# Summing, norming and multiplying each tile of tokens on its own between two transformer blocks

## The chip, the cores and the metric

The kernel runs on one core of a Trainium2 chip. The metric is the device time of one execution in microseconds (us), the median of several runs. The engines are named as the profile names them: PE (TensorE, matmuls), PEld (its weight loads), DVE (VectorE), ACT (ScalarE), POOL (GpSimd) and SP (SyncE, which issues the DMAs here). Each engine works through its own instructions in order and waits for others at semaphores.

## What is computed

The program is two transformer blocks over 512 tokens of width 1024: a block with two attentions and a mixture of experts, then a block with three other attentions and an MLP. All of it is float32. What matters here lies between the two blocks:

```python
    x = x + gate_f * moe_ffn(h, ...)          # end of the first block
    return rms_norm(x, g_final)
...
    h = rms_norm_2(x, norm_mix[l])            # start of the second block
    proj = h @ w_in[l]
```

where both norms are `x * rsqrt(mean(x*x) + 1e-6) * gain`. So x is normed twice in a row, and the result is multiplied by `w_in`.

## The kernel before

Tokens lie in four tiles of 128 (the variable `c` or `i`). The residual x is `xres`, four tiles of 128x1024 in SBUF. Products that need precision are written as three matmuls in a rounded format (`mm3`, lines 121 to 123): a value is kept as a rounded part `hi`, made by ACT (line 88), and a remainder `lo`, made by DVE (line 89); the matmuls are hi*hi, hi*lo and lo*hi. Of a weight these parts are the tiles `whi` and `wlo`, three buffers each; the raw weights are loaded by SP into `raw`, three buffers.

The experts are worked off in slots (the loop of `phase_b`). For each slot the program makes y, 128 rows of expert output, as `yh` and `yl` (line 1073 multiplies by the gate, lines 88 and 89 split), and a selection matrix S. `combine` (lines 1084 to 1094) adds S^T y to `xres`: for each tile and each half of 512 columns it runs two matmuls per slot into one PSUM bank and one addition on DVE. Of the last two slots the sums are made in `tail`. The last slot's y lies in a buffer named `rawh`, so its products read `rawh`; its matmuls of line 1071 work on four experts of 32 rows.

`tail` takes the tiles in pairs. It sums both, squares them on ACT (line 1486) and weights the squares on DVE (line 1488), finds both norms' scales with a Newton iteration in small DVE instructions (lines 1490 to 1495, 262 to 267), multiplies each tile by its scale and gains (line 1499), turns it by eight PE transposes (line 1504) and splits it into `c_hh` and `c_hl`. The four instructions of line 1510 write the normed x back. The products with the first 396 columns of `w_in_2` come later, in `nsa_kv` of `phase_c`: for each quarter of the 1024 rows of the weight it runs over all four tiles. Then ACT and DVE read them (`kvc`, `kvt`, `ksw`, `gt`), PE turns `ksw` (line 1667), and the query's products (`nsa_q`, lines 121 to 123 on `c_hh` with 512 columns) follow. Masks and gains are loaded into `mkf`, `gains` and others at the start of `phase_c`.

A scheduler sets each engine's order when the program is built, from its own estimate of when each instruction is ready. `order(a, b)` forces b behind a on the same engine. `pe` does that for every matmul that is passed to it while `self.chain` is a list; so PE's order in the expert loop is the order of the code.

Of the kernel before, what the change touches and what calls it, by code (L numbers as in the profile page):

```python
# [11 lines left out]
F32 = mybir.dt.float32  # L12
F32R = mybir.dt.float32r
# [45 lines left out]
class Kern:  # L59
# [750 lines left out]
    NB = sum(k[0] for k in KINDS)  # L810
# [284 lines left out]

    def phase_b(self):
        nc, tc, I = self.nc, self.tc, self.I
        xr, hT, hp = self.xres, self.h2T, self.hp
        E, STAT, NB, NS, NF = self.E, self.STAT, self.NB, self.NS, self.NF
# [57 lines left out]
        for j in range(3):  # L1157
            t = rt.tile([128, D], F32, name=f"xg{j}")
# [13 lines left out]
        for c in range(NCH):  # L1172
# [4 lines left out]
                                       op0=OP.add, op1=OP.mult)  # L1177
# [56 lines left out]
        for name, src in (("pos", pos), ("gate", sco)):  # L1234
            t = self.tps()
# [4 lines left out]
            t = self.tps()  # L1240
# [72 lines left out]
        n = 2  # L1313
        while todo:
            p = todo[0]
# [4 lines left out]
            n = 3  # L1320
# [144 lines left out]
        self.gains = g[:, :D], g[:, D:]  # L1465
        self.rowcast(self.gains[0], I["g_final"].rearrange("(o d) -> o d", o=1))
        self.rowcast(self.gains[1], I["norm_mix_2"])
        nc.gpsimd.tensor_tensor(self.gains[1], self.gains[0], self.gains[1], op=OP.mult)

        nc.gpsimd.tensor_tensor(self.gff, self.gains[0], self.gains[0], op=OP.mult)  # L1470
        self.done, self.ex = done, ex
        bwx.close()

    def tail(self):

        nc, xr, hT = self.nc, self.xres, self.cT
        gfin, gmix = self.gains
        G = 2
        sq2, xn2 = [self.hold.tile([128, self.RAW], F32, name="rawh", bufs=self.NP) for _ in range(2)]
        for a in range(0, NCH, G):  # L1480
            self.combine(self.done, range(a, a + G))
            st = self.nst[:, a * 6:(a + G) * 6].rearrange("p (s n) -> p s n", s=6)
            xs = [xr[:, a + j, :] for j in range(G)]
            for j in range(G):
                sq = sq2[:, (a + j) % 2 * D:][:, :D]
                d = nc.scalar.activation(sq, xs[j], AF.Square, accum_out=st[:, 0, j:j + 1])
                self.order(self.pin, d)
                nc.vector.scalar_tensor_tensor(sq, sq, 1.0, self.gff, op0=OP.mult, op1=OP.mult, accum_out=st[:, 1, j:j + 1])

            nc.vector.tensor_scalar(st[:, 0], st[:, 0], 1.0 / D, EPS, op0=OP.mult, op1=OP.add)  # L1490
            nc.vector.reciprocal(st[:, 2], st[:, 0])
            nc.vector.scalar_tensor_tensor(st[:, 1], st[:, 1], 1.0 / D, st[:, 2], op0=OP.mult, op1=OP.mult)
            nc.vector.tensor_scalar(st[:, 1], st[:, 1], EPS, None, op0=OP.add)
            self.rsqrt(st[:, 4:6], st[:, 0:2], st[:, 2:4])
            nc.vector.tensor_tensor(st[:, 0], st[:, 4], st[:, 5], op=OP.mult)
            for j in range(G):
                i = a + j
                xn = xn2[:, i % 2 * D:][:, :D]
                self.fence = nc.vector.scalar_tensor_tensor(xn, xs[j], st[:, 0, j:j + 1], gmix, op0=OP.mult, op1=OP.mult)
                for h in range(2):  # L1500
                    t = self.tps()
                    for k in range(4):
                        kk = 4 * h + k
                        nc.tensor.transpose(t[:, k * 128:(k + 1) * 128], xn[:, kk * 128:(kk + 1) * 128], self.ident)
                    sl = (slice(None), slice(4 * h, 4 * h + 4), slice(i * 128, (i + 1) * 128))
                    self.split(t.rearrange("p (k n) -> p k n", k=4), hT.hi[sl], hT.lo[sl])
            if a == 0:
                self.fence0 = self.fence
# [60 lines left out]
    def phase_c(self):  # L1569
# [65 lines left out]

        def nsa_kv():

            N = 396
            kvt = ap.tile([128, 4, 128], F32, name="kvt")
            kvc, ksw = [ap.tile([128, 512], F32, name=n, tag="PTd", bufs=3).rearrange("p (c n) -> p c n", c=4)  # L1640
                        for n in ("kvc", "ksw")]
            gt = ap.tile([128, 4, 12], F32, name="gt")
            raws = [self.load_w(w, 256, N, 4 * h, 4) for h in range(2)]
            ps = [self.acc() for _ in range(NCH)]
            for q in range(4):
                wb = self.split_w(raws[q // 2][:, 2 * (q % 2):2 * (q % 2) + 2], self.fence0 if q >= 0 else None)
                for k in range(2):
                    kk = 2 * q + k
                    for c in range(NCH):
                        cc = slice(c * 128, (c + 1) * 128)  # L1650
                        self.mm3(ps[c][:, :N], hT.hi[:, kk, cc], hT.lo[:, kk, cc], wb.hi[:, k], wb.lo[:, k],
                                 kk == 0, kk == KC - 1)
# [505 lines left out]
```

## Time and profile before

| | |
|---|---|
| median of 3 runs | 1721.33 us (1721.08, 1721.33, 1730.81) |
| profiled execution | 1720.41 us, its span 1718.7 us |
| mean granted TensorE clock | 0.995 of 2.4 GHz |
| busy | PE 97%, PEld 66%, DVE 57%, ACT 34%, POOL 4% |
| chain of waits that ended last | PE 89%, DVE 5%, DMA 3%, ACT 2%, issue 1% |

Times in the text are us from the span's start. In the profile a matmul's duration overlaps that of the next, so the distance between two starts is what one costs. In square brackets stands how long the engine had been idle before an instruction, and what ended that. A granted clock of 1.00 is 2.4 GHz and 0.50 is 1.2 GHz.

### The profile page before, as it was taken

The page shows a single profiled execution, that of the slowest core. Times are in us where ns is not written, and L with a number is a line of the kernel's source. Part 1 is how long each engine was busy: PE and PEld are TensorE (multiplying, and loading weights), DVE is VectorE, ACT ScalarE, POOL GpSimd, SP SyncE. Part 2 cuts the span into 40 slices and gives each one's busy share as a digit, 9 for nine tenths or more (in the row PEclk, how much of TensorE's full clock was granted, in tenths as well). Part 3 has the DMA queues.
Part 4 walks back from the last instruction along what each step waited for, and adds up shares of the span by engine and source line. Part 5 has one row for each costly group of instructions (what it writes and reads, how often), then busy time and mean ns, then how long its engine had stood idle before and what let it go on. Part 6 is the DMA issues. An engine that isn't in the chain of part 4 may idle for free.

```text
span 1718.7 us, 23490 instructions
## 1 busy us (share of the span) xinstructions
PE 1674.0 (97%) x8740; PEld 1125.9 (66%) x8743; DVE 971.1 (57%) x1915; ACT 584.9 (34%) x1123; POOL 65.8 (4%) x96
## 2 busy tenths in 40 slices
PE   7999999999999999999999979999999999999999
PEld 2767776788854444544544448667756888888887
DVE  5685646367755656656566568565446744234422
ACT  3555454424211111111111134455456443124311
POOL 0000000001011000000000010000000000000000
PEclk9999999999999999999999999999999999999999
DMA  9333426237879999999999945101202432323230
GB/s 306 115 99 99 126 96 201 69 123 302 326 293 369 408 397 405 409 394 407 392 408 402 406 146 150 37 25 62 74 1 74 123 98 98 98 74 98 99 123 25
DMA packets 137893, 341.88 MB, mean 199 GB/s; under 512 B 12986, under 2 KB 59389, under 8 KB 137775
## 3 DMA queue, kind: packets, MB, share of 16 engines
q1 hardware_dynamic: 133168, 327.76, 51.9%
q0 software_dynamic: 4608, 12.59, 1.9%
q8 instruction: 70, 1.15, 0.3%
q14 instruction: 47, 0.39, 0.1%
HBM read 340.26 MB, written 4.21 MB: 200 GB/s over the span
## 4 chain that ended last, share of the span: by engine, by line
PE 89%; DVE 5%; DMA 3%; ACT 2%; issue 1%; SPq 0%; DVEq 0%; POOLq 0%; POOL 0%; ACTq 0%
PE acc L121 15%; PE acc L123 14%; PE acc L122 14%; PE acc L1047 12%; PE acc L1071 6%; PE acc L1093 3%; PE acc L1092 3%; PE t L1032 2%; PE s L323 2%; PE t L296 2%; PE po L332 2%; PE s L1832 1%; PE acc L1456 1%; PE po L1842 1%; PE s L1860 1%
## 5 line engine op out<-in xcount | busy, mean ns | idle before, releaser
L89 DVE TENSOR_TENSOR wlo<-raw,whi 128x1024 fp32r<-128x1024 f32 (+4 forms) x162 | 189.6, 1172 | 243.1 <-ACT whi L88 241.7
L88 ACT ACTIVATE whi<-raw 128x1024 fp32r<-128x1024 f32 (+4 forms) x162 | 164.6, 1019 | 254.2 <-PE acc L123 163.8
L1094 DVE TENSOR_TENSOR xres<-xres,acc 128x512 f32<-128x512 f32 x248 | 151.3, 682 | 0.5 <-PE acc L1093 0.5
L1047 PE MATMUL acc<-raw,xT 128*32 128x512 f32 (+2 forms) x760 | 147.0, 594 | 0.5 <-DMA raw<-in_w_exp_up_dram 0.4
L121 PE MATMUL acc<-m_hh,whi 128*128 128x512 f32 (+1 forms) x272 | 104.0, 384 | 2.0 <-ACT m_hh L88 2.0
L123 PE MATMUL acc<-m_hh,wlo 128*128 128x512 f32 (+1 forms) x272 | 104.5, 384 | 0.0
L122 PE MATMUL acc<-m_hl,whi 128*128 128x512 f32 (+1 forms) x272 | 104.4, 384 | 0.0
L1092 PE MATMUL acc<-yh,S 128*128 128x512 f32 x248 | 103.0, 415 | 0.0
L88 ACT ACTIVATE yh<-yg 128x512 fp32r<-128x512 f32 x62 | 39.1, 630 | 184.0 <-DVE yg L1073 184.0
L123 PE MATMUL acc<-whi,ul 128*128 128x512 f32 x256 | 101.1, 395 | 0.0
L122 PE MATMUL acc<-wlo,uh 128*128 128x512 f32 x256 | 101.1, 395 | 0.0
L121 PE MATMUL acc<-whi,uh 128*128 128x512 f32 x256 | 101.1, 395 | 0.0
L1050 DVE SCALAR_TENSOR_TENSOR hs<-hs,gate,acc 128x256 f32<-128x256 f32 x32 | 15.4, 481 | 149.6 <-ACT hs L1049 149.6
L1047 PEld LDWEIGHTS acc<-raw,xT 128*32 128x32 f32 (+2 forms) x760 | 47.9, 123 | 76.7 <-issue 70.3
L1093 PE MATMUL acc<-yl,S 128*128 128x512 f32 x248 | 97.6, 393 | 0.0
L1071 PE MATMUL acc<-wlo,hT 128*32 128x512 f32 (+2 forms) x272 | 91.1, 596 | 1.0 <-ACT hT L1059 1.0
L1047 PE MATMUL acc<-rawh,xT 128*32 128x512 f32 (+2 forms) x408 | 83.1, 594 | 0.3 <-issue 0.3
L121 PE MATMUL acc<-hh,whi 128*128 128x512 f32 x176 | 73.9, 420 | 0.0
L1049 ACT ACTIVATE hs<-acc 128x256 f32<-128x256 f32 x32 | 12.3, 384 | 176.3 <-PE acc L1047 176.3
L123 PE MATMUL acc<-hh,wlo 128*128 128x512 f32 x176 | 70.5, 400 | 0.0
L122 PE MATMUL acc<-hl,whi 128*128 128x512 f32 x176 | 70.0, 398 | 0.0
L286 DVE TENSOR_REDUCE st<-s 128x1 f32<-128x128 f32 (+1 forms) x96 | 46.4, 486 | 36.3 <-PE s L324 20.6
(634 smaller groups left out, 3540.4 us busy)
## 6 DMA issues: line engine op xcount, KB each, us to landing
raw<-in_w_exp_gate_dram SPq DMA_DIRECT2D x70, 512.0 KB
raw<-in_w_exp_up_dram SPq DMA_DIRECT2D x70, 512.0 KB
whi<-in_w_exp_down_dram SPq DMA_DIRECT2D x48, 512.0 KB
wlo<-in_w_exp_down_dram SPq DMA_DIRECT2D x48, 512.0 KB
raw<-in_w_in_dram SPq DMA_DIRECT2D x21, 1024.0 KB
rawh<-in_w_exp_gate_dram SPq DMA_DIRECT2D x36, 512.0 KB
rawh<-in_w_exp_up_dram SPq DMA_DIRECT2D x36, 512.0 KB
raw<-in_w_mod_dram SPq DMA_DIRECT2D x16, 1024.0 KB
```

Of the source, the lines that this page charges most:

```text
L88: self.nc.scalar.activation(hi, src, AF.Copy)
L89: return self.nc.vector.tensor_tensor(lo, src, hi.bitcast(F32), op=OP.subtract)
L121: mm(out, lh, rh, start=start, stop=False)
L122: mm(out, lh, rl, start=False, stop=False)
L123: mm(out, ll, rh, start=False, stop=stop)
L286: nc.vector.tensor_reduce(st[:, 1:2], s_ps[:, :n], axis=AX.X, op=OP.max, negate=True)
L296: nc.tensor.transpose(t[:, kb * 128:(kb + 1) * 128], P[:, kb * 128:(kb + 1) * 128], self.ident)
L1047: self.pe(nc.tensor.matmul(pg[a:b].rearrange("p (u n) -> p u n", u=2), xT[:, kk, a:b], ws[kk // 4][:, kk % 4], start=(kk == 0), stop=(kk = ...
L1071: self.pe(nc.tensor.matmul(p[a:b], hT[:, j, a:b], ws[2 + j][:, s], start=(j == 0), stop=(j == 1)))
L1092: self.pe(nc.tensor.matmul(p, l, y.hi[:, s], start=(i == 0), stop=False))
L1093: self.pe(nc.tensor.matmul(p, l, y.lo[:, s], start=False, stop=(i == len(done) - 1)))
L1094: nc.vector.tensor_tensor(xr[:, c, s], xr[:, c, s], p, op=OP.add)
```

## The change

The sums of the last two slots, the two norms and the products with the 396 columns are done tile by tile. The bank of tile 0 gets its matmuls for the slot before the last already inside the expert loop (`partial`), ahead of the last slot's own products. The tile is multiplied by the first gain (`xg`), and both squares are now sums on ACT; one root, of EPS times the first sum plus the second, gives the scale of the doubly normed tile: a logarithm and an exponential on ACT, and one Newton step of four small DVE instructions. The products of a tile follow its own transposes; PE's order there is the code's, by `pe`, and so is DVE's, by the new `dve`. ACT's is left to the scheduler. The remainder of a weight's quarter is placed by `low`. The fourth quarter's two parts lie in a `raw` buffer. The four instructions that write back the normed x move from DVE to ACT, behind a root for all four tiles. Two multiplications on POOL are gone.

```diff
@@ phase_b, in the loop over slots
+            if i == NB - 1:
+                self.banks = {}
+                for h in range(2):
+                    self.partial(0, h, *done[0], 0, self.sps)
...
-        nc.gpsimd.tensor_tensor(self.gains[1], self.gains[0], self.gains[1], op=OP.mult)
-
-        nc.gpsimd.tensor_tensor(self.gff, self.gains[0], self.gains[0], op=OP.mult)
+    def partial(self, c, h, S, y, i, bank):
+
+        if i == 0:
+            self.banks[c, h] = bank()
+        p, s, l = self.banks[c, h], slice(h * 512, (h + 1) * 512), S[:, c * 128:(c + 1) * 128]
+        self.pe(self.nc.tensor.matmul(p, l, y.hi[:, s], start=(i == 0), stop=False))
+        self.pe(self.nc.tensor.matmul(p, l, y.lo[:, s], start=False, stop=(i == 1)))
+    def dve(self, d):
+
+        if self.dchain:
+            self.order(self.dchain[-1], d)
+        self.dchain = [d]
+        return d
@@ tail
+        for q in range(4):
+            if q < 3:
+                hi, lo = self.hilo(2 * N)
+            else:
+                r = self.raw(2048).bitcast(F32R)
+                hi, lo = r[:, :2 * N], r[:, D:D + 2 * N]
...
+            nc.scalar.activation(hi, src, AF.Copy)
...
+        def low(q):
+            lo, src, hi = lows[q]
+            dve(v.tensor_tensor(lo, src, hi.bitcast(F32), op=OP.subtract))
...
+        def square(c):
+
+            sq = tl.tile([128, D], F32, name="sq", bufs=1)
+            d = nc.scalar.activation(sq, xr[:, c, :], AF.Square, accum_out=st[:, 0, c:c + 1])
+            self.order(self.pin, d)
+            dve(v.tensor_tensor(xg[c], xr[:, c, :], gfin, op=OP.mult))
+            nc.scalar.activation(sq, xg[c], AF.Square, accum_out=st[:, 1, c:c + 1])
+
+        def root(c, a, b, bias):
+
+            l = tl.tile([128, NCH], F32, name="ln", bufs=2)
+            n = c.stop - c.start
+            nc.scalar.activation(l[:, :n], st[:, a, c], AF.Ln, bias=bias, scale=1.0 / D)
+            nc.scalar.activation(st[:, b, c], l[:, :n], AF.Exp, scale=-0.5)
...
+        def stat(c):
+
+            c1 = slice(c, c + 1)
+            dve(v.scalar_tensor_tensor(st[:, 2, c1], st[:, 0, c1], EPS, st[:, 1, c1], op0=OP.mult, op1=OP.add))
+            root(c1, 2, 3, eps2)
+
+        def normed(c):
+            newton(slice(c, c + 1), 2, 3, EPS * EPS)
+            xn = tl.tile([128, D], F32, name="xn", bufs=2)
+            dve(v.scalar_tensor_tensor(xn, xg[c], st[:, 3, c:c + 1], gmix, op0=OP.mult, op1=OP.mult))
+            turned_[c] = xn
...
+        def products(c):
+            cc = slice(c * 128, (c + 1) * 128)
+            p = self.acc()[:, :N]
+            for kk in range(KC):
+                wb, k = wbs[kk // 2], kk % 2
+                pe(mm(p, hT.hi[:, kk, cc], wb.hi[:, k], start=(kk == 0), stop=False))
+                pe(mm(p, hT.hi[:, kk, cc], wb.lo[:, k], start=False, stop=False))
+                pe(mm(p, hT.lo[:, kk, cc], wb.hi[:, k], start=False, stop=(kk == KC - 1)))
+            self.kvp.append(p)
...
+        low(0)
+        add(0, 0)
+        add(0, 1)
+        square(0)
+        add(1, 0)
+        add(1, 1)
+        stat(0)
+        square(1)
+        normed(0)
+        add(2, 0)
+        add(2, 1)
...
+        stat(1)
+        low(1)
+        turned(0)
+        normed(1)
+        low(2)
+        low(3)
+        products(0)
+        square(2)
+        turned(1)
+        add(3, 0)
+        add(3, 1)
+        stat(2)
+        square(3)
+        products(1)
+        normed(2)
+        turned(2)
+        stat(3)
+        products(2)
+        normed(3)
+        turned(3)
+        products(3)
+        self.chain = None
+        al = slice(0, NCH)
+        root(al, 0, 4, self.eps)
+        newton(al, 0, 4, EPS)
+        for c in range(NCH):
+            nc.scalar.activation(xr[:, c], xg[c], AF.Copy, scale=st[:, 4, c:c + 1])
@@ nsa_kv
-            raws = [self.load_w(w, 256, N, 4 * h, 4) for h in range(2)]
-            ps = [self.acc() for _ in range(NCH)]
-            for q in range(4):
...
+            ps = self.kvp
```

On PE, at the last slot: `ht` are the transposes of the slots' hidden values, line 1070 (1071 before) the expert's output, s the banks of tile 0. This is the order now; before, the row of the second `ht` was followed at once by `wlo,hT`:

```order
L1056 MATMUL ht<-ident,hs 128x128 x2
L1100 MATMUL s<-yh,S 128x512
L1101 MATMUL s<-yl,S 128x512
L1100 MATMUL s<-yh,S 128x512
L1101 MATMUL s<-yl,S 128x512
L1070 MATMUL acc<-wlo,hT 32x512 x2
L1070 MATMUL acc<-rawd,hT 32x512
```

Four matmuls that read the slot before the last moved ahead of the last slot's products.

On ACT, the squares and roots of the first tiles (`sq,nst` are squares with their sums, `ln` the logarithms, `nst<-ln` the exponentials, `c_hh` the rounded halves of a turned tile), as they now stand:

```order
L1537 ACTIVATE sq,nst<-xres 128x1024
L1540 ACTIVATE sq,nst<-rawh 128x1024
L1537 ACTIVATE sq,nst<-xres 128x1024
L1546 ACTIVATE ln<-nst,eps_9229 128x1
L1540 ACTIVATE sq,nst<-rawh 128x1024
L1547 ACTIVATE nst<-ln 128x1
L1579 ACTIVATE c_hh<-t 128x4x128
L1546 ACTIVATE ln<-nst,eps_9229 128x1
L1537 ACTIVATE sq,nst<-xres 128x1024
L1547 ACTIVATE nst<-ln 128x1
L1579 ACTIVATE c_hh<-t 128x4x128
L1540 ACTIVATE sq,nst<-xb 128x1024
```

Before, four squares and then eight `c_hh` stood here; now each root of a tile has a square of the next tile in between.

On ACT again, the end of the stage, before:

```order
L88 ACTIVATE c_hh<-t 128x4x128 x8
L88 ACTIVATE whi<-raw 128x792
L88 ACTIVATE whi<-raw 128x1024 x2
L1654 ACTIVATE kvc<-acc 128x128 x2
L1657 ACTIVATE kvt<-acc 128x128
```

and now:

```order
L1579 ACTIVATE c_hh<-t 128x4x128 x2
L88 ACTIVATE whi<-raw 128x1024
L1634 ACTIVATE xres<-rawh,nst 128x1024 x2
L1634 ACTIVATE xres<-xb,nst 128x1024 x2
L88 ACTIVATE whi<-raw 128x1024
L1768 ACTIVATE kvc<-acc 128x128 x4
```

The write-back of four tiles came in between the two weight roundings of the query. DVE follows there with the remainders of both, and only behind the second with the `ksw` that PE waits for:

```order
L1554 SCALAR_TENSOR_TENSOR nst<-nst 128x4
L89 TENSOR_TENSOR wlo<-raw,whi 128x1024
L1712 MEMSET bd 128x128
L1738 TENSOR_SCALAR smask<-before 128x128
L1740 TENSOR_SCALAR ntri<-before 128x128
L1713 MEMSET bd 64x64
L1714 MEMSET bd 64x64
L1742 TENSOR_SCALAR nones<-ones 128x128
L1842 MEMSET misc 128x31
L89 TENSOR_TENSOR wlo<-raw,whi 128x1024
L1770 COPY ksw<-acc 128x128 x3
```

## Rows read from the trace of the kernel before

**Rows 1.** Windows: busy us of PE, PEld, DVE, ACT, POOL (instructions); clock; DMA share; GB/s

```profile
1015.00:1023.00 8.00, 0.00 (x0) 0.00 (x0) 8.00 (x38) 2.30 (x4) 0.00 (x0) 0.82 0.00 0
1031.00:1039.00 8.00, 8.00 (x51) 7.54 (x50) 7.96 (x10) 2.70 (x5) 0.00 (x0) 1.00 0.09 30
1047.00:1063.00 16.00, 15.57 (x67) 10.66 (x68) 11.56 (x27) 7.58 (x14) 0.00 (x0) 1.00 1.03 306
```

**Rows 2.** Timeline of PE: start, us, engine, line, names, shapes, count [idle before <-what ended it]

```profile
1002.29 0.62 PE L1071 MATMUL acc<-wlo,hT 128*32 128x512 f32 x2 [0.99 <-ACT hT L1059]
...
1005.86 0.50 PE L1092 MATMUL acc<-yh,S 128*128 128x512 f32 x1
...
1009.88 0.50 PE L1093 MATMUL acc<-rawh,S 128*128 128x512 f32 x1 [1.00 <-DVE rawh L89]
1010.22 0.39 PE L1092 MATMUL acc<-yh,S 128*128 128x512 f32 x1
1010.45 0.40 PE L1093 MATMUL acc<-yl,S 128*128 128x512 f32 x1
...
1014.60 0.39 PE L1093 MATMUL acc<-rawh,S 128*128 128x512 f32 x1
1023.11 1.97 PE L1504 MATMUL t<-ident,rawh 128*128 128x128 f32 x8 [8.12 <-DVE rawh L1499]
...
1031.93 1.03 PE L1504 MATMUL t<-ident,rawh 128*128 128x128 f32 x8
...
1046.31 0.34 PE L123 MATMUL acc<-whi,c_hl 128*128 128x396 f32 x1
1046.49 0.53 PE L1667 MATMUL t<-ident,ksw 128*128 128x128 f32 x2
...
1048.63 0.33 PE L1667 MATMUL t<-ident,ksw 128*128 128x128 f32 x1 [0.43 <-DVE ksw L1656]
```

**Rows 3.** Timeline of DVE, the last two slots' remainders and the first normed pair

```profile
1003.54 0.69 DVE L89 TENSOR_TENSOR yl<-yg,yh 128x512 fp32r<-128x512 f32 x1 [1.35 <-ACT yh L88]
...
1007.91 1.92 DVE L89 TENSOR_TENSOR rawh<-yg,rawh 128x512 fp32r<-128x512 f32 x1
...
1021.77 2.48 DVE L1499 SCALAR_TENSOR_TENSOR rawh<-xres,nst,rawh 128x1024 f32<-128x1024 f32 x2
```

**Rows 4.** Timeline of POOL beside them

```profile
1007.39 1.89 POOL L1470 TENSOR_TENSOR gff<-rawh 128x1024 f32<-128x1024 f32 x1 [70.48 <-DVE yg L1073]
```

**Rows 5.** Groups of DVE, 1009 to 1050, by form: busy us, mean ns | idle before

```profile
L89 DVE TENSOR_TENSOR c_hl<-t,c_hh 128x512 fp32r<-128x512 f32 x8 | 5.4, 689 | 0.3 <-ACT c_hh L88 0.3
...
L1499 DVE SCALAR_TENSOR_TENSOR rawh<-xres,nst,rawh 128x1024 f32<-128x1024 f32 x4 | 5.0, 1282 | 0.0
...
L1094 DVE TENSOR_TENSOR xres<-xres,acc 128x512 f32<-128x512 f32 x7 | 4.7, 682 | 0.5 <-PE acc L1093 0.5
L89 DVE TENSOR_TENSOR wlo<-raw,whi 128x792 fp32r<-128x792 f32 x4 | 3.9, 977 | 0.0
L89 DVE TENSOR_TENSOR wlo<-raw,whi 128x1024 fp32r<-128x1024 f32 x3 | 3.7, 1223 | 0.5 <-ACT whi L88 0.5
...
L267 DVE SCALAR_TENSOR_TENSOR nst<-nst 128x4 f32<-128x4 f32 x6 | 0.9, 160 | 0.0
```

**Rows 6.** Groups of ACT, 1009 to 1100, by form

```profile
L88 ACT ACTIVATE whi<-raw 128x1024 fp32r<-128x1024 f32 x8 | 8.5, 1059 | 7.8 <-PE acc L122 5.9 <-PE acc L123 1.9
L88 ACT ACTIVATE c_hh<-t 128x512 fp32r<-128x512 f32 x8 | 4.7, 598 | 13.9 <-PE t L1504 13.8
L1486 ACT ACTIVATE rawh<-xres 128x1024 f32<-128x1024 f32 x4 | 4.2, 1055 | 6.1 <-DVE xres L1094 6.1
...
L1486 ACT ACTIVATION_READ_ACCUMULATOR rawh<-xres 128x1 f32 x4 | 0.7, 185 | 0.0
...
L1542 ACT ACTIVATE qsq<-misc 128x31 f32<-128x31 f32 x1 | 0.2, 229 | 0.5 <-DVE misc L1729 0.5
```

**Rows 7.** Windows of 1 us (columns as in Rows 1)

```profile
1020.00:1021.00 1.00, 0.00 (x0) 0.00 (x0) 1.00 (x12) 0.00 (x0) 0.00 (x0) 0.60 0.00 0
...
1027.00:1028.00 1.00, 1.00 (x8) 0.87 (x8) 0.74 (x2) 0.88 (x2) 0.00 (x0) 0.99 0.00 0
```

**Rows 8.** SP: issues of DMAs; and what SP waited for, 1000 to 1075

```profile
1027.46 0.38 SPq L106 DMA_DIRECT2D raw<-in_w_in_dram  x1
1040.30 0.74 SPq L1593 DMA_DIRECT2D gains<-in_qk_gain_nsa_dram  x1
...
SPq L1593 <- DVE xres L1510: 11.8, 1, 11.8
```

More of the change, by code (lines that the diff above doesn't have):

```diff
@@ L790, in open_mid @@
         self.gff = mp.tile([128, D], F32, name="gff")
-        self.nst = mp.tile([128, 6 * NCH], F32, name="nst")
     def ffn_mod(self):
@@ L1467, in phase_b @@
         self.rowcast(self.gains[1], I["norm_mix_2"])
-        nc.gpsimd.tensor_tensor(self.gains[1], self.gains[0], self.gains[1], op=OP.mult)
-        nc.gpsimd.tensor_tensor(self.gff, self.gains[0], self.gains[0], op=OP.mult)
         self.done, self.ex = done, ex
         bwx.close()
+    def dve(self, d):
[3 more added lines that the diff above has]
+        return d
     def tail(self):
         nc, xr, hT = self.nc, self.xres, self.cT
+        v, mm, pe, dve = nc.vector, nc.tensor.matmul, self.pe, self.dve
+        done, banks = self.done, self.banks
@@ L1477, in tail @@
         gfin, gmix = self.gains
[L1478 to L1508, printed above, removed]
@@ L1509, in tail @@
-        for i in range(NCH):
-            d = nc.vector.scalar_tensor_tensor(xr[:, i], xr[:, i], self.nst[:, 20 + i % 2 - 12 * (i < 2):][:, :1], gfin, op0=OP.mult, op1=OP.mult)
-            self.order(self.fence, d)
+        tlx = ExitStack()
+        tl = tlx.enter_context(self.tc.tile_pool(name="tl", bufs=1, side="right"))
+        st = tl.tile([128, 6, NCH], F32, name="nst")
+        eps2 = tl.tile([128, 1], F32, name="eps2")
+        nc.gpsimd.memset(eps2, EPS * EPS)
+        xa = self.hold.tile([128, self.RAW], F32, name="rawh", bufs=self.NP)
@@ new lines, in tail @@
+        xb = tl.tile([128, 2 * D], F32, name="xb")
+        xg = [t[:, j * D:(j + 1) * D] for t in (xa, xb) for j in range(2)]
+        N = 396
+        w = self.I["w_in_2"][0]
+        raws = [self.load_w(w, 256, N, 4 * h, 4) for h in range(2)]
+        self.kvp, wbs, lows, turned_ = [], [], [], {}
+        self.chain, self.dchain = [], []
+        for q in range(4):
[4 more added lines that the diff above has]
+                hi, lo = r[:, :2 * N], r[:, D:D + 2 * N]
+            hi, lo = [t.rearrange("p (k n) -> p k n", n=N) for t in (hi, lo)]
+            src = raws[q // 2][:, 2 * (q % 2):2 * (q % 2) + 2]
+            nc.scalar.activation(hi, src, AF.Copy)
+            lows.append((lo, src, hi))
+            wbs.append(Split(hi, lo))
@@ new lines, in low, with summed, add @@
+        def low(q):
+            lo, src, hi = lows[q]
+            dve(v.tensor_tensor(lo, src, hi.bitcast(F32), op=OP.subtract))
+        def summed(c, h, i):
+            self.partial(c, h, *done[i], i, self.acc if 0 < c < 3 else self.sps)
+        def add(c, h):
+            s = slice(h * 512, (h + 1) * 512)
+            dve(v.tensor_tensor(xr[:, c, s], xr[:, c, s], banks.pop((c, h)), op=OP.add))
+        def square(c):
[4 more added lines that the diff above has]
+            nc.scalar.activation(sq, xg[c], AF.Square, accum_out=st[:, 1, c:c + 1])
@@ new lines, in root, with newton @@
+        def root(c, a, b, bias):
[3 more added lines that the diff above has]
+            nc.scalar.activation(st[:, b, c], l[:, :n], AF.Exp, scale=-0.5)
+        def newton(c, a, b, add):
+            t = st[:, 5, c]
+            dve(v.tensor_scalar(st[:, a, c], st[:, a, c], -0.5 / D, -0.5 * add, op0=OP.mult, op1=OP.add))
+            dve(v.tensor_tensor(t, st[:, b, c], st[:, b, c], op=OP.mult))
+            dve(v.tensor_tensor(t, t, st[:, a, c], op=OP.mult))
+            dve(v.scalar_tensor_tensor(st[:, b, c], t, 1.5, st[:, b, c], op0=OP.add, op1=OP.mult))
@@ new lines, in stat, with turned @@
+        def stat(c):
[7 more added lines that the diff above has]
+            turned_[c] = xn
+        def turned(c):
+            ts = []
+            for h in range(2):
+                t = self.tps()
+                for k in range(4):
+                    kk = 4 * h + k
+                    pe(nc.tensor.transpose(t[:, k * 128:(k + 1) * 128], turned_[c][:, kk * 128:(kk + 1) * 128], self.ident))
+                ts.append((t, h))
+            for t, h in ts:
+                sl = (slice(None), slice(4 * h, 4 * h + 4), slice(c * 128, (c + 1) * 128))
+                t = t.rearrange("p (k n) -> p k n", k=4)
+                nc.scalar.activation(hT.hi[sl], t, AF.Copy)
+                dve(v.tensor_tensor(hT.lo[sl], t, hT.hi[sl].bitcast(F32), op=OP.subtract))
@@ new lines, in products @@
+        def products(c):
[7 more added lines that the diff above has]
+            self.kvp.append(p)
+        for c, h, i in ((1, 0, 0), (1, 1, 0), (0, 0, 1), (1, 0, 1), (2, 0, 0), (2, 1, 0), (0, 1, 1), (1, 1, 1), (2, 0, 1), (2, 1, 1)):
+            summed(c, h, i)
@@ new lines, in tail @@
+        low(0)
[9 more added lines that the diff above has]
+        add(2, 1)
+        for h in range(2):
+            for i in range(2):
+                summed(3, h, i)
+        stat(1)
[10 more added lines that the diff above has]
+        stat(2)
@@ L1512, in tail @@
+        square(3)
[13 more added lines that the diff above has]
+            nc.scalar.activation(xr[:, c], xg[c], AF.Copy, scale=st[:, 4, c:c + 1])
+        tlx.close()
         self.ex.close()
@@ L1636, in nsa_kv @@
         def nsa_kv():
-            N = 396
             kvt = ap.tile([128, 4, 128], F32, name="kvt")
@@ L1642, in nsa_kv @@
             gt = ap.tile([128, 4, 12], F32, name="gt")
-            raws = [self.load_w(w, 256, N, 4 * h, 4) for h in range(2)]
-            ps = [self.acc() for _ in range(NCH)]
-            for q in range(4):
[L1646 to L1652, printed above, removed]
+            ps = self.kvp
             for c in range(NCH):
```

## The prediction

> **What bounds the kernel now.** The order of every engine is the same before and behind the stage between the blocks, so only that stage can move the time, and I read it in four views.
>
> The chain of waits puts 89% of the end on PE: what counts is how long PE stands still, or works slowly, in this stage. The timeline of PE [rows 2] is to show where. Until 1014.8 it sums the last slots, with idle of 0.99 before the last slot's narrow products at 1002.29 and of 1.00 at 1009.88, where it waits for the remainder `rawh`. Then it waits 8.12 for the first normed tile. From 1023.11 to 1046.5 it works with hardly a break: first transposes, then the products. Only 0.43 is lost at the last transpose of `ksw`. That makes 0.99 + 1.00 + 8.12 + 0.43 = 10.5 us of idle time.
>
> The windows show what PE waits for: between 1015 and 1023 DVE is busy 8.00 of 8 us [rows 1]. The clock's row has it at 0.60 in 1020 to 1021, and it is back at 0.99 in 1027 to 1028 [rows 7]; eight transposes cost 1.97 at first and 1.03 later [rows 2], so half rate costs about 2 us more. Thus **the change can win 12.6 us at most**, 0.7%. From 1047 to 1063 PE is busy 15.57 of 16 us [rows 1], and no DMA paces it there: a delay in this stage is not given back later.
>
> **The change step by step.** I stepped through the new order of PE, ACT, DVE and SP, each instruction starting when its engine is free and its inputs are there, with the durations of the rows. For the kernel before the same stepping ends at 1046.2 where the trace has 1046.5, so I trust it to some tenths for known rows.
>
> *Last slot.* Four matmuls of tile 0 now stand ahead of the narrow products, and the last needs the second half of `yl`. That ends at 1003.54 + 0.69 = 1004.23 [rows 3]; with one matmul of 0.23 [rows 2] the narrow products start near 1004.5, not 1002.29: 2.2 later. Their results take 7.54 more until the remainder is complete (1002.29 to 1007.91 + 1.92 = 1009.83). Of this 1.92, 1.23 goes: it ran beside POOL's multiplication [rows 4], which is removed, and without it a remainder takes 0.69 [rows 5]. So 1004.5 + 6.3 = 1010.8, by the stepping 1011.1 (before 1009.8). Two matmuls and an addition of 0.68 [rows 5] later, tile 0 is summed at 1012.5.
>
> *Tile 0's scale.* ACT squares 1.06 with 0.19 to read the sum [rows 6], DVE makes `xg` beside it (as a line-1499 multiplication, 1.28 [rows 5]), ACT squares that: 1015.1 with `stat`. But ACT's order has tile 1's first square ahead of the logarithm and its second ahead of the exponential: 2 x 1.24. The exponential ends at 1017.7, four small DVE steps of 0.16 to 0.2 [rows 5] at 1018.4, `xn` at 1019.7. PE turns tile 0 at **1019.7, 3.4 before the old 1023.11**, having stood idle 4.9. No row has a logarithm of one column; the nearest, 128x31, takes 0.23 [rows 6]. I take that, between 0.16 and 0.29 (six on the path, so 0.4 either way).
>
> *Products.* One tile costs PE 1.03 for transposes and 24 matmuls of 0.18, some 4.35: 5.4 [rows 2]. Four take 21.6, so PE could end at 1041.3. It can't, since DVE's order is the code's: the remainders `low(2)` and `low(3)` of the weight, 0.98 each [rows 5], which tile 0's products need, stand behind `normed(1)`. Ahead of it are tile 2's additions (until 1020.9), `low(1)` (1021.8) and tile 0's own two remainders (1023.7, the second waiting for ACT, which squares between the halves). `xn(1)` ends at 1025.6, `low(3)` at 1027.5, and tile 0's products at 1028.6: waits of 0.3, 1.1 and 2.1. Tile 1 loses 1.2 to a square of tile 2 between its two `c_hh`, and ends at 1035.2. Tile 2's `xn` is ready only at 1037.6: its exponential stands behind tile 3's square, and additions and `xg` of tile 3 stand before it on DVE. PE waits 2.5 and ends at 1043.7; tile 3 ends at 1049.8. Before it was 1046.5: **+3.3**.
>
> *Behind the products.* ACT has left: `whi` 1.0, the four write-backs, 0.97 apart as full rows of 1024 columns go, another `whi`, which ends at 1052.6; DVE's `wlo` of 1.22 [rows 5] stands ahead of the last `ksw`. PE's transposes of `ksw` start near 1054.0, after 4.2 of waiting where it was 0.43: **+3.8**.
>
> *Constants and buffers.* The fourth quarter's parts hold a `raw` buffer until tile 3's products end. SP's third load of `w_in_2`, issued at 1027.46 before, then waits until 1050, and behind it on SP's queue stand gains and masks, issued from 1040.30 on [rows 8]. That brings 0.4 at `kvt`, 1.9 at the block-diagonal products (the square of q takes the buffer that the mask's cast must free) and 1.8 at the compressed keys, which miss a `whi` buffer. Low end 0.4, high end 4.1. I take **3.0**, nearer the high end, as SP's order is fixed while how fast the late transfers land is open.
>
> *Nothing:* the two POOL multiplications of 1.89 free POOL, on which nobody waits but through the remainder counted above. The write-backs leave DVE, on no path; their price is the one on ACT.
>
> **Sum:** 3.3 + 3.8 + 3.0 = +10.1 on the profiled 1720.41: 1730.5. The median lies 0.9 above that execution, so 1731. With the bounds of the unknown costs (0.4 for small ACT steps, 2.6 below and 1.1 above for the constants, 1.5 for a clock that stays at half until 1030) the likeliest case is 1728 to 1734.
>
> **The rivals.**
>
> *Not slower.* The tiles fill the pipe as it is meant: transposes and products back to back from 1019.7. Then products end at 1041.3, 5.2 earlier than before and 8.5 before my sum; the `ksw` wait stays, since ACT's load is the same, less what starts earlier; with constants at 0.4 the sum is -5.2 + 3.8 + 0.4 = -1.0, so **1720**. It decides whether `xn(1)` comes before 1023.6 and `xn(2)` before 1031. Against it: DVE was full for 8 us [rows 1], and the order now puts other tiles' additions and weight remainders ahead. For it: PE's sums for tiles 1 to 3 are as early as before, and my durations on a crowded DVE may be too long. Chance 0.15.
>
> *The clock falls.* PE stood idle from 1014.8 and the clock read 0.60 at 1020 [rows 7]; it came back only after PE had worked nearly unbroken from 1023.1. Now idle times of 4.9, 2.1 and 2.5 are spread through the stage. If all four tiles ran at half rate, their 21.6 would double; 8.5 of idle within the stage and 4.2 of the `ksw` wait would take up some, which leaves +8.9. With half of them, some +5. I put this case at 1735 to 1740 (1730.5 + 0.9, and 4 to 8.9 more). Against it: the first idle time is shorter than the 8.12 of before, after which the clock came back in 4 us. Chance 0.13.
> The Trainium skill ("TensorE: Matmul & The Clock Gate", section "HAM oscillation — how this bites in real kernels") says that repeated waits between short groups of matmuls bring the half rate back again and again. By that rule the time would be near 1739; the rows before show one fall and no repetition, so they do not bear it out yet.
>
> *The constants come late.* Loads behind the third of `w_in_2` take longer than I took, since 16 weight packets go ahead of each on the same engines (DMA share 1.03 in 1047 to 1063 [rows 1]): +2, **1733**. Chance 0.07.
>
> **How the numbers follow.** My sum has 0.65, the rivals 0.15, 0.13 and 0.07. The likeliest time is 1731. For 8 in 10, the range goes from the not-slower case at 1720 to the middle of the clock's case, 1737. Faster or slower by 1% (1704 and 1738.5), about what a measurement of this kernel can tell from no change: the first is beyond the 12.6 us that could be won and gets 0.01; the second needs most of the clock's case, 0.07; the rest, 0.92, is within.
>
> **What the changed profile would show.** The narrow products start near 1004.5 and the remainder `rawh` takes 0.7. The first transposes come near 1019.7, after 4.9 of idle time that ends with DVE's `xn`. Tile 0's products wait for `low`, and tile 2's transposes about 2.5 for `xn`. The last product ends near 1050, the `ksw` transposes wait some 4 for DVE, and SP issues its third load near 1050. I am wrong if products run without a break from 1020; if the clock is under 0.8 over several windows of 1020 to 1050; or if ACT's write-backs are done before the last products are.

## The result, and the profile after

| | before | after |
|---|---|---|
| median of 11 runs each | 1725.77 us | 1742.55 us |
| lowest to highest | 1720.38 to 1730.81 | 1731.00 to 1745.53 |
| profiled execution, its span | 1720.41, 1718.7 | 1735.89, 1734.2 |
| mean granted clock | 0.995 | 0.992 |
| busy: PE, PEld, DVE, ACT, POOL | 97%, 66%, 57%, 34%, 4% | 97%, 65%, 56%, 34%, 4% |
| chain of waits: PE, DVE, DMA, ACT, issue | 89%, 5%, 3%, 2%, 1% | 89%, 5%, 2%, 3%, 1% |

The changed kernel is slower: the ratio is 1.0087, with an interval of 1.0066 to 1.0107. That is 15 us, where I had forecast 10, and the median lies above the range that I gave. The changed kernel's times are five from 1731.00 to 1735.89 and six from 1742.55 to 1745.53, so its median is one of the longer ones; the five shortest of each kernel have the middle values 1721.08 and 1734.49, which is 13.4 us.

To leave out what varies elsewhere, I measure the stage itself: from the start of the last slot's `ht` transposes to the first score of the compressed keys. Before:

```profile
1000.86 0.44 PE L1057 MATMUL ht<-ident,hs 128*128 128x128 f32 x2
...
1082.51 1.01 PE L1797 MATMUL s<-kc,qa 66*128 66x31 f32 x8
```

After:

```profile
1001.58 0.44 PE L1056 MATMUL ht<-ident,hs 128*128 128x128 f32 x2
...
1096.19 0.99 PE L1911 MATMUL s<-kc,qa 66*128 66x31 f32 x8
```

The stage is 1082.51 - 1000.86 = 81.65 us before and 1096.19 - 1001.58 = 94.61 after, 12.96 longer. The rest of the span grew by 2.5, of which more below.

PE's timeline after the change, with the columns of [rows 2]:

```profile
1004.24 0.51 PE L1100 MATMUL s<-yh,S 128*128 128x512 f32 x1 [1.55 <-ACT yh L88]
1004.96 0.50 PE L1101 MATMUL s<-yl,S 128*128 128x512 f32 x1 [0.22 <-DVE yl L89]
1005.39 0.62 PE L1070 MATMUL acc<-wlo,hT 128*32 128x512 f32 x2
...
1010.66 0.50 PE L1100 MATMUL acc<-yh,S 128*128 128x512 f32 x1
...
1022.05 1.97 PE L1574 MATMUL t<-ident,xn 128*128 128x128 f32 x8 [4.61 <-DVE xn L1565]
...
1029.09 0.45 PE L1588 MATMUL acc<-wlo,c_hh 128*128 128x396 f32 x1 [1.31 <-DVE wlo L1525]
...
1031.19 1.03 PE L1574 MATMUL t<-ident,xn 128*128 128x128 f32 x8
...
1039.95 1.83 PE L1574 MATMUL t<-ident,xn 128*128 128x128 f32 x8 [2.14 <-DVE xn L1565]
...
1052.85 0.34 PE L1589 MATMUL acc<-raw,c_hl 128*128 128x396 f32 x1
1057.80 0.87 PE L1781 MATMUL t<-ident,ksw 128*128 128x128 f32 x3 [4.62 <-issue]
...
1075.32 0.38 PE L1819 MATMUL acc<-w,craw 128*32 128x128 f32 x2 [1.57 <-issue]
```

Where PE had one long wait of 8.12 and two of 1.0 [rows 2], it now has four of 1.8 to 4.6 us (the first is split in two, 1.55 and 0.22) and some short ones. They stand where the prediction had them: before tile 0's second half, before its transposes, before tile 2's, and before `ksw`'s. New is the duration of what follows each. The narrow products take 10.66 - 5.39 = 5.27 where they took 3.57, and eight transposes take 1.97 and 1.83 behind waits but 1.03 behind products. The windows around those four places say why (columns as in [rows 1]; the last but two is the clock). The first line is the single fall before, the others are after:

```profile
1020.00:1028.00 8.00, 4.89 (x22) 4.15 (x23) 7.74 (x28) 2.08 (x4) 0.00 (x0) 0.57 0.01 2
...
1005.00:1010.00 5.00, 5.00 (x29) 1.44 (x33) 0.71 (x2) 1.32 (x2) 0.00 (x0) 0.66 0.19 76
1019.00:1027.00 8.00, 4.95 (x18) 4.26 (x19) 5.79 (x15) 3.49 (x9) 0.00 (x0) 0.57 0.20 63
1040.00:1044.00 4.00, 4.00 (x16) 3.53 (x17) 1.75 (x5) 1.92 (x6) 0.00 (x0) 0.57 0.00 0
1057.00:1061.00 4.00, 3.20 (x11) 2.69 (x12) 3.74 (x16) 1.82 (x6) 0.00 (x0) 0.57 0.65 170
```

A mean of 0.57 over 4 us means that 2 x (1 - 0.57) x 4 = 3.4 of them were at half rate. The four windows hold 17 us at half rate, against some 7 in the single fall before. In some 2.6 of the 17, and 2.9 of the 7, PE was still waiting.

ACT's timeline around the roots and behind the last products:

```profile
1018.53 0.28 ACT L1546 ACTIVATE ln<-nst,eps 128x1 f32<-128x1 f32 x1
1018.85 1.06 ACT L1540 ACTIVATE sq<-rawh 128x1024 f32<-128x1024 f32 x1
1019.91 0.19 ACT L1547 ACTIVATE nst<-ln 128x1 f32<-128x1 f32 x1
...
1053.02 2.17 ACT L1634 ACTIVATE xres<-xb,nst 128x1024 f32<-128x1024 f32 x2
1055.10 1.04 ACT L88 ACTIVATE whi<-raw 128x1024 fp32r<-128x1024 f32 x1
```

A square of tile 1 runs between tile 0's logarithm and exponential, and the write-backs run where `ksw` is waited for, both as predicted. What the write-backs hold is seen on DVE and SP:

```profile
1055.34 0.17 DVE L1712 MEMSET bd<- 128x128 f32 x1 [3.05 <-ACT xres L1634]
...
1056.17 1.22 DVE L89 TENSOR_TENSOR wlo<-raw,whi 128x1024 fp32r<-128x1024 f32 x1
1057.31 0.68 DVE L1770 COPY ksw<-acc 128x128 f32<-128x128 f32 x3
```

```profile
1055.26 0.74 SPq L1717 DMA_DIRECT2D gains<-in_qk_gain_nsa_dram  x1
```

The second `whi` stands behind the write-backs, its remainder `wlo` behind that, and `ksw` behind the remainder: this is PE's wait of 4.62. The next phase's first write to its own memory (`bd`) waits for the last write-back, which ends at 1053.02 + 2.17 = 1055.19, and so does the load of gains, issued at 1040.30 before [rows 8]. In the code the pools of tiles that `tail` works on are closed behind the write-backs, and the next phase opens its own after that; which buffer's memory is waited for isn't shown.

### The profile page after: what moved, and what is told of

Its sections match the earlier page's. It is cut to its first block, busy times and chain, and to the rows that moved or that the text cites. A ratio compares the mean times of both kernels' runs of the same rounds, so it can differ in the third digit from the quotient of the medians.

```text
span 1734.2 us, 23493 instructions
## 1 busy us (share of the span) xinstructions
PE 1681.5 (97%) x8740; PEld 1126.4 (65%) x8743; DVE 965.7 (56%) x1899; ACT 594.1 (34%) x1145; POOL 61.1 (4%) x95
## 4 chain that ended last, share of the span: by engine, by line
PE 89%; DVE 5%; ACT 3%; DMA 2%; issue 1%; SPq 0%; ACTq 0%; POOL 0%; POOLq 0%; DVEq 0%
PE acc L121 14%; PE acc L123 14%; PE acc L122 14%; PE acc L1046 13%; PE acc L1070 6%; PE acc L1091 3%; PE acc L1092 3%; PE t L1031 2%; PE s L323 2%; PE t L296 2%; PE po L332 2%; PE s L1946 1%; PE acc L1467 1%; PE s L1974 1%; PE po L1956 1%
## 5 line engine op out<-in xcount | busy, mean ns | idle before, releaser
L89 DVE TENSOR_TENSOR wlo<-raw,whi 128x1024 fp32r<-128x1024 f32 (+3 forms) x158 | 185.6, 1176 | 245.9 <-ACT whi L88 244.5
L88 ACT ACTIVATE whi<-raw 128x1024 fp32r<-128x1024 f32 (+3 forms) x158 | 161.0, 1022 | 253.8 <-PE acc L123 160.6
L1093 DVE TENSOR_TENSOR xres<-xres,acc 128x512 f32<-128x512 f32 x240 | 145.8, 678 | 0.0
```

Of the source, the lines that this page charges most:

```text
L88: self.nc.scalar.activation(hi, src, AF.Copy)
L89: return self.nc.vector.tensor_tensor(lo, src, hi.bitcast(F32), op=OP.subtract)
```

## The experiments

In all but the last two, one thing is changed against the changed kernel, so 94.61 is the number to compare with. "Stage" is the stretch defined above, read from one profile of each version. The falls of the clock differ in two of these profiles, the third and the sixth, at places that the edit doesn't touch; what that does to the reading is said there.

**The early matmuls of tile 0 put back.**

```diff
-            if i == NB - 1:
-                self.banks = {}
-                for h in range(2):
-                    self.partial(0, h, *done[0], 0, self.sps)
...
-        for c, h, i in ((1, 0, 0), (1, 1, 0), ...
+        for c, h, i in ((0, 0, 0), (0, 1, 0), (1, 0, 0), (1, 1, 0), ...
```

> The four matmuls of tile 0 go back behind the last slot's narrow products; nothing else is changed against the changed kernel. I measure the stage from the last slot's ht transposes to the first score of the compressed keys: 81.65 us in the kernel before, 94.61 in the changed one. Theory 1 (PE's wait for yh and yl delays the narrow products and lets the clock fall on them): the narrow products start near 1003.0 instead of 1005.4 and take 3.6 instead of 5.3; the stage is 90 to 92. Rival (the later steps on DVE and ACT set the pace anyway): the narrow products are earlier, but the stage stays at 93.5 or more.

Stage 91.53, ratio to the kernel before 1.0046 (1.0023 to 1.0069). PE's timeline:

```profile
1000.97 0.62 PE L1070 MATMUL acc<-wlo,hT 128*32 128x512 f32 x2 [0.63 <-ACT hT L1058]
...
1004.54 0.50 PE L1100 MATMUL s<-yh,S 128*128 128x512 f32 x1
```

The narrow products start 1.72 after `ht` (3.81 in the changed kernel) and take 3.57. Theory 1 holds: the early matmuls brought 2.1 us of waiting and 1.7 of half rate, and 3.1 of that reach the end of the stage.

**The root for the write-backs early.**

```diff
         normed(3)
+        al = slice(0, NCH)
+        root(al, 0, 4, self.eps)
+        newton(al, 0, 4, EPS)
+        for c in range(NCH):
+            nc.scalar.activation(xr[:, c], xg[c], AF.Copy, scale=st[:, 4, c:c + 1])
         turned(3)
         products(3)
         self.chain = None
-        al = slice(0, NCH)
...
```

> The root for all four tiles, its Newton step and the four write-backs on ACT stand ahead of tile 3's transposes in the code instead of behind its products. Theory 1 (the late write-backs hold ACT, and with it DVE's ksw copies, the memory that the next phase needs, and so SP's loads of gains and masks): the ksw transposes wait under 2 us instead of 4.6, the first load of gains is issued before 1050 instead of 1055.3, and the stage falls from 94.6 to between 88 and 91. Rival, as the prediction had it (the raw buffer of the fourth quarter holds SP until tile 3's products end): the gains' load stays behind 1052, the wait at the block-diagonal products stays, and the stage falls by 3 at most, to 92 or more.

Stage 90.40, ratio 1.0048 (1.0026 to 1.0069). Of PE, ACT and SP in this kernel, in turn:

```profile
1049.57 0.70 PE L1587 MATMUL acc<-whi,c_hh 128*128 128x396 f32 x1 [2.92 <-ACT c_hh L1579]
...
1055.43 0.49 PE L1781 MATMUL t<-ident,ksw 128*128 128x128 f32 x3
```

```profile
1046.86 2.17 ACT L1631 ACTIVATE xres<-xb,nst 128x1024 f32<-128x1024 f32 x2
```

```profile
1049.10 0.74 SPq L1717 DMA_DIRECT2D gains<-in_qk_gain_nsa_dram  x1
```

The wait before `ksw`'s transposes is gone, and gains are issued right after the last write-back (1046.86 + 2.17 = 1049.03), 1049.10 - 1000.26 = 48.8 after `ht` and not 53.7. Theory 1 holds for what the write-backs hold. One more thing differs, though: a load of `w_in_2` that SP issued ahead of gains comes behind them here (1062.74), so for gains this run alone doesn't tell the raw buffer from the write-backs; the sixth does. The write-backs now stand ahead of tile 3's `c_hh`, which costs PE a new wait of 2.92; in all, 4.2 us are won.

**ACT's order: each root ahead of the next tile's squares.**

```diff
-            nc.scalar.activation(st[:, b, c], l[:, :n], AF.Exp, scale=-0.5)
+            self.aexp = nc.scalar.activation(st[:, b, c], l[:, :n], AF.Exp, scale=-0.5)
...
-            self.order(self.pin, d)
+            self.order(self.aexp if c else self.pin, d)
```

> On ACT each tile's logarithm and exponential are forced ahead of the next tile's squares. Theory 1 (ACT's order delays the normed tiles): tile 0's transposes start 1.4 to 2.5 us earlier than 22.05 - 1.58 = 20.5 us after the last slot's ht, tile 2's wait of 2.1 shrinks, and the stage falls to 89 to 92. Rival (DVE's fixed order is what holds, ACT's is covered): the stage stays at 94 to 95.

Stage 90.25, ratio 1.0053 (1.0029 to 1.0077). PE's timeline:

```profile
1003.59 0.62 PE L1070 MATMUL acc<-wlo,hT 128*32 128x512 f32 x2
...
1007.16 0.50 PE L1100 MATMUL acc<-yh,S 128*128 128x512 f32 x1
...
1017.15 1.09 PE L1574 MATMUL t<-ident,xn 128*128 128x128 f32 x8 [3.21 <-DVE xn L1565]
...
1033.37 1.06 PE L1574 MATMUL t<-ident,xn 128*128 128x128 f32 x8 [0.74 <-DVE xn L1565]
```

Tile 0's transposes start 1017.15 - 999.55 = 17.60 after `ht` (20.47 in the changed kernel), tile 2's wait falls from 2.14 to 0.74, and eight transposes take 1.06 there instead of 1.83. Theory 1 holds, but not all of the 4.4 us is the order's. The narrow products, which come ahead of anything that the edit moves, take 3.57 here and 5.27 in the changed kernel: the clock stays at 1.00 on them, though PE waits as it did there (1.78 and 0.22). Counted from their end, tile 0's transposes come 1017.15 - 1007.16 = 9.99 later where it was 11.39, so 1.4 are the order's on that tile. On the other side the fall around `ksw` lasts 7 us here and 3.4 in the changed kernel. What the order left to the scheduler cost in all is thus known to some 1.7 us either way.

**Matmuls without use in PE's waits.**

```diff
-                    self.partial(0, h, *done[0], 0, self.sps)
+                    self.partial(0, h, *done[0], 0, self.sps, 8 * h)
...
+        for _ in range(warm):
+            self.pe(self.nc.tensor.matmul(p, l, y.hi[:, :512], start=True, stop=True))
...
                 t = self.tps()
+                for _ in range({0: 16, 2: 8}.get(c, 0) * (1 - h)):
+                    pe(mm(t, done[0][0][:, :128], done[0][1].hi[:, :512], start=True, stop=True))
...
             t = self.tps()
+            for _ in range(16):
+                d = nc.tensor.matmul(t, hT.hi[:, 0, 0:128], hT.hi[:, 0, :], start=True, stop=True)
+                self.order(self.plast, d)
```

> 48 matmuls of 512 columns whose results are overwritten stand in PE's four long waits of the changed kernel (8 ahead of the second half of tile 0, 16 ahead of its transposes, 8 ahead of tile 2's, 16 ahead of ksw's); the order of the rest is the same. Theory 1 (the four falls of the clock, to 0.50, come from these waits and cost 3 to 5 us in all): the granted clock stays at 1.00 through the stage, the narrow products take 3.6, eight transposes 1.03 everywhere, and the stage falls to 90 to 92. Rival (the half-rate stretches lie beside waits for DVE and ACT and cost nothing): the clock stays up, but the stage is 94 to 95. Second rival (the added matmuls themselves delay PE): 95 or more.

Stage 90.51, ratio 1.0046 (1.0026 to 1.0066). Windows:

```profile
1006.00:1008.00 2.00, 2.00 (x22) 0.64 (x24) 0.00 (x0) 0.40 (x1) 0.00 (x0) 1.00 0.31 125
...
1024.00:1026.00 2.00, 2.00 (x6) 2.00 (x7) 1.90 (x6) 0.22 (x3) 0.00 (x0) 0.50 0.77 231
...
1038.00:1040.00 2.00, 1.70 (x10) 1.14 (x10) 0.69 (x2) 1.09 (x2) 0.00 (x0) 1.00 0.00 0
1056.00:1058.00 2.00, 2.00 (x11) 1.65 (x10) 1.80 (x6) 0.28 (x2) 0.00 (x0) 1.00 0.75 236
```

With every dependency and every order as in the changed kernel, and work added to PE, the stage is 4.1 us shorter: that much its clock cost, or more, since one fall is left. Three of the four falls are gone. The other comes later, in 1023 to 1027, behind waits of under 1 us each (0.99, 0.25, 0.79), so a long wait is not the only thing that brings one; theory 1 holds but for this.

**`low(2)` and `low(3)` ahead of `normed(1)`.**

```diff
-        normed(1)
         low(2)
         low(3)
+        normed(1)
```

> The weight remainders low(2) and low(3) stand ahead of normed(1) on DVE instead of behind it; nothing else is changed against the changed kernel. Theory 1 (the prediction's step: tile 0's products wait for them): the wait of 1.3 us at line 1588 goes, tile 1's transposes come no earlier than normed(1) allows, and the stage from the last slot's ht to the first score of the compressed keys falls from 94.6 to 93 to 94. Rival (DVE is the bound, the order only moves the wait): a wait of over 1 us stands ahead of tile 1's transposes instead, and the stage stays at 94.3 or more.

Stage 94.01, ratio 1.0059 (1.0036 to 1.0082). The wait at line 1588 is gone and none stands ahead of tile 1's transposes, as theory 1 has it, but 0.6 us is all that the step was worth, less than the wait itself: tile 2's transposes still wait 2.14 for DVE.

**A buffer of its own for the fourth quarter's parts.**

```diff
-                r = self.raw(2048).bitcast(F32R)
-                hi, lo = r[:, :2 * N], r[:, D:D + 2 * N]
+                r = tl.tile([128, 4 * N], F32, name="w3").bitcast(F32R)
+                hi, lo = r[:, :2 * N], r[:, 2 * N:]
```

> The two parts of the weight's fourth quarter get a buffer of their own instead of one of the three raw buffers. Theory 1 (what the second experiment points to: the constants wait for memory that the write-backs hold, not for the raw buffer): the third load of w_in_2 is issued before 1035 instead of 1053, but the first load of gains still near 1055, and the stage stays at 93.5 to 94.6. Rival (the prediction's account of the constants): gains are issued soon after 1040, the waits behind the ksw transposes go, and the stage falls to 91 or 92.

Stage 94.58, ratio 1.0077 (1.0046 to 1.0109). SP's issues, a window, and PE behind `ksw`:

```profile
1022.09 5.87 SPq L106 DMA_DIRECT2D raw<-in_w_in_dram  x2
1052.76 0.74 SPq L1717 DMA_DIRECT2D gains<-in_qk_gain_nsa_dram  x1
```

```profile
1054.00:1062.00 8.00, 6.24 (x15) 3.86 (x16) 5.57 (x19) 3.30 (x10) 0.00 (x0) 0.57 0.62 169
```

```profile
1059.64 1.90 PE L1668 MATMUL t<-qsq,bd 128*128 128x512 f32 x2 [0.46 <-ACT qsq L1666]
```

SP is free of the raw buffer from 1028 on and still issues gains at 1052.76, right behind the last write-back (1052.69) and 53.5 us after `ht` as in the changed kernel (53.7). So my account falls for gains and masks: the write-backs hold them, not the raw buffer. It doesn't fall for the compressed keys. PE's wait of 1.57 ahead of them, which the first, third and fifth experiments have too (1.54 to 1.63), is gone; 0.46 is all that PE waits behind `ksw`. That the stage is no shorter goes with the clock, which is at half rate for 2 x (1 - 0.57) x 8 = 6.9 us around `ksw` and not for 3.4. That the raw buffer cost nothing is therefore not shown.

**Both orders written out anew.** The same operations as in the changed kernel, with ACT in a fixed order too, and tile 0's early matmuls back behind the narrow products. Of the sequence, for tiles 0 and 1 and for the end, in short names and not as the code has it (`xg` is the first gain's multiplication, `sqa` and `sqb` the squares, `xn` the normed tile, `tr` its transposes, `hi` and `lo` the two parts of a split, `wnewt` and `wb` the write-backs' root and the write-backs):

```diff
+ add:0:0 low:1 add:0:1 xg:0 sqa:0 low:2 sqb:0 sum3 add:2:1 stat:0 add:1:0 root:0 newt:0 add:1:1 xn:0
+ sqa:1 add:2:0 tr:0 xg:1 hi:0:0 wroot:0:2 hi:0:1 lo:0:0 sqb:1 xg:2 stat:1 lo:0:1 prod:0 root:1 sqb:2 newt:1 xn:1
...
+ wnewt:2:4 newt:3 xn:3 wb:0 wb:1 wb:2 wb:3 tr:3 hi:3:0 hi:3:1 lo:3:0 lo:3:1 prod:3
```

> The changed kernel with the orders of DVE and ACT both written out anew for the stage: exponentials ahead of the next tile's squares, weight remainders in DVE's idle times, sums of the next tile ahead of a tile's splits, both roots for the write-backs early and all write-backs ahead of tile 3's splits; tile 0's early matmuls go back behind the narrow products. Theory 1 (the change lost by its order, not by its idea of working by tiles): products end near 39 us after the last slot's ht (46 in the kernel before, 51 in the changed one), the stage is 76 to 80 against 81.65 before, and the time is 2 to 5 us below the kernel before. Rival (waits between tiles keep the clock low and DVE has no room): the stage is 82 to 86 and the time no better than before.

Stage 77.88, ratio 0.9988 (0.9967 to 1.0009). PE's timeline:

```profile
1015.20 1.09 PE L1580 MATMUL t<-ident,xn 128*128 128x128 f32 x8 [3.57 <-DVE xn L1573]
...
1022.62 1.04 PE L1580 MATMUL t<-ident,xn 128*128 128x128 f32 x8
...
1028.72 1.04 PE L1580 MATMUL t<-ident,xn 128*128 128x128 f32 x8
...
1034.81 1.03 PE L1580 MATMUL t<-ident,xn 128*128 128x128 f32 x8
...
1044.41 0.33 PE L1833 MATMUL t<-ident,ksw 128*128 128x128 f32 x1 [0.64 <-DVE ksw L1822]
```

This is the pipe of the "not slower" rival: the tiles follow each other by 7.4, 6.1 and 6.1 us, and none of the last three waits ahead of its transposes. Products end 41.6 after `ht` (45.6 before), and the stage is 3.8 shorter than before. In the stage, the work by tiles was not what lost the time; its order was. The time as a whole can't be told from the kernel before, so the 2 to 5 us below it that I expected are not shown.

**The same, with 13 matmuls without use ahead of tile 0's transposes.**

```diff
                 t = turns[c, h] = self.tps()
+                for _ in range(13 if c == h == 0 else 0):
+                    pe(mm(t, done[0][0][:, :128], done[0][1].hi[:, :512], start=True, stop=True))
```

> The same with 13 matmuls whose results are overwritten ahead of tile 0's transposes, in a wait of some 3.9 us. Theory 1 (that wait is what lets the clock fall on the transposes and products behind it): the granted clock stays at 1.00 from 1010 to 1035, and the stage is 1 to 3 us shorter than without them. Rival (the fall has to do with more than this wait): the clock falls somewhere in the stage all the same and the stage is within 0.7 us of the one without them.

Stage 77.98, ratio **0.9970 (0.9948 to 0.9993)**, median 1716.40 of 12 runs against 1722.05: the one version here whose interval lies below 1, by a little. A window, PE, and DVE:

```profile
1010.00:1040.00 30.00, 27.67 (x148) 23.99 (x147) 25.04 (x64) 22.79 (x48) 0.17 (x2) 1.00 0.24 71
```

```profile
1040.81 0.49 PE L1835 MATMUL t<-ident,ksw 128*128 128x128 f32 x3
1045.51 0.33 PE L1835 MATMUL t<-ident,ksw 128*128 128x128 f32 x1 [1.48 <-DVE ksw L1824]
```

```profile
1042.81 0.43 DVE L1784 CAST mk<-mkf 128x512 bf16<-128x512 f32 x1 [1.36 <-DMA mkf<-in_cst_dram]
```

The clock stays at 1.00, as theory 1 has it, and products end 40.7 after `ht`, 0.9 earlier. But the stage is no shorter, as the rival has it, for another reason than the rival gave: DVE now waits for the masks, and the last `ksw` waits behind their casts (PE waits 1.48 for it, not 0.64). That the whole is faster than without these matmuls isn't shown; the two intervals overlap.

## Why the prediction was wrong

The direction and the places were right, the size was not. By its own steps, with times counted from `ht`:

- *Last slot.* Narrow products 2.2 later: 3.81 after `ht` instead of 1.43, so 2.4. The remainder `rawh` takes 0.69 without POOL's multiplication beside it, as costed. Not foreseen: the products themselves, 1.7 longer at half rate.
- *Tile 0's scale.* Transposes were to come 3.4 earlier; relative to `ht` they come at 20.47 instead of 22.25, so 1.8. The difference is the 1.7 of the narrow products.
- *Products.* They were to end 3.3 later; the last starts 51.3 after `ht` where 45.5 was before, so 5.8. The 1.7 is in it again, and the half rate on tiles 0 and 2. With matmuls put into the waits (fourth experiment) it starts at 47.75, so 2.3 later than before.
- *Behind the products.* A wait of 4.2 was forecast, 4.62 came, and its cause is as given, by the second experiment.
- *Constants.* From the last `ksw` transpose to the first score the changed kernel takes 1096.19 - 1058.90 = 37.3, the kernel before 1082.51 - 1048.63 = 33.9: 3.4 for the 3.0 that I took. That the size came out is in part luck. The wait of 1.57 at the compressed keys is the 1.8 of the sum, and goes with the `raw` buffer (sixth experiment); the 1.9 at the block-diagonal products left no wait on PE; some 0.8 is half rate behind `ksw`, where four matmuls from 1058.97 take 1.73 and would take 0.93. Gains and masks came late because of the write-backs, not of the `raw` buffer (second and sixth). [rows 8] had it: the wait of 11.8 stands there as one for line 1510, the write-backs of the kernel before. The 16 packets of the last rival no run shows; the trace before counts 1040 for that 1024 KB load.

The step that failed is the clock. I put every matmul of the stage at full rate in the sum and gave the falling clock 0.13, with the argument that the first wait is shorter than the 8.12 of before. A shorter wait did not spare it: behind 4.61, behind 2.14, behind 4.62, and behind 1.55 and 0.22 together the clock fell, and 17 us of the stage passed at half rate. What that cost is 4.1 by the fourth experiment, where I had zero. In that experiment the stage is 8.9 longer than before, where I had 10.1: the waits alone I had 1.2 too long, and the clock turned that into 2.9 too short.

The trace of the kernel before had the repetition that I missed, further back than my rows go:

```profile
1302.08 0.44 PE L1949 MATMUL sbC<-sp,nones 128*128 128x128 f32 x2 [1.96 <-DVE sbe L1932]
...
1360.60 0.97 PE L121 MATMUL acc<-m_hh,whi 128*128 128x256 f32 x4 [2.00 <-ACT m_hh L88]
```

```profile
1302.00:1308.00 6.00, 5.92 (x27) 5.28 (x28) 5.72 (x14) 5.88 (x14) 0.00 (x0) 0.72 0.00 0
```

Behind waits of 1.96 and 2.00 the clock stood at half rate for 3.4 us each time (the second window, 1360 to 1366, has 0.72 too). The Trainium skill ("TensorE: Matmul & The Clock Gate", section "HAM oscillation — how this bites in real kernels") describes half rate coming back with each round of waiting; the trace of the changed kernel agrees, with four falls. But such a wait doesn't bring a fall in every execution: behind 1.78 and 0.22 in the third experiment, and behind the same 1.96 in the seventh, the clock stayed at 1.00.

A second term was mis-sized, the step from the profiled execution to the median. I took 0.9 from three runs; with eleven the median lies 5.4 above the profiled execution before (1725.77 - 1720.41) and 6.7 above it after. That, and not the stage alone, took the median past 1737: the profiled 1735.89 is within the range.

So the stage cost 13.0 where I had 10.1. The other 2.5 of the profiled difference lies outside the stage, where the order of the instructions is the same, and where such differences come without the change: span less stage is 1637.05 before and 1639.59 after, but also 1636.5 in the first experiment, 1635.9 in the sixth and 1644.8 in the third. A part of it, 1.7 at most, is a stretch of 3.4 us at half rate in 101 to 105, which of the ten profiles only this one and that of the fourth experiment have.

The single costs don't simply add up: 3.1 for the early matmuls, 4.2 for the late write-backs, 4.4 for ACT's order and 4.1 for the clock are 15.8, and the 1.7 of half rate on the narrow products is in the first, the third and the fourth of them. The version that mends the first three and the place of the weight remainders is 16.7 shorter.

## What to carry to other kernels

When one engine's order is fixed by hand and another's is left to a scheduler, look at the places where the two meet: here squares of the next tile, put ahead of a logarithm and its exponential, made the first tile 1.4 us late. When a long wait of TensorE is cut into several short ones, look through the whole trace before for what the clock did behind waits of that length, and cost the matmuls behind each at half rate until a trace shows otherwise. And ask of the last reader of a stage's memory what the next stage wants to load there.

## What the runs showed of the hardware

- **A long stretch at half rate in some executions.** The profile of the third experiment (span 1735.0) has some 17 us at half rate, from 1120 to 1137, and that of the seventh from 1108 to 1125, far behind the stage, while PE works:

```profile
1120.00:1137.00 17.00, 17.00 (x59) 10.74 (x58) 7.19 (x23) 4.90 (x14) 0.00 (x0) 0.52 0.01 1
```

  A wait of 1.19 ends shortly ahead of it in both (at 1119.62 in the third), but all ten profiles have that wait, and the other eight have no such stretch. At half rate 17 us of PE's work take the place of 8.5; outside the stage the third experiment's span is 8.3 longer than the first's (1644.75 for 1636.47). What brings the stretch is open.
- **Root of one column.** The logarithm of a 128x1 tile takes 0.28 and the exponential 0.19 on ACT, about the 0.23 of 31 columns [rows 6].
